# Projections of a gated mLSTM and convolution layer: pairs of tiles by seven block products, all ahead of the mLSTM

## The chip, the cores and the metric

The kernel runs on one core of one Trainium2 chip. The metric is the device time of one execution in microseconds (us); lower is better. Engines: PE (TensorE, matmuls), DVE (VectorE), ACT (ScalarE), POOL (GpSimd), SP (SyncE, issues most DMAs). All data is float32.

## The reference

One layer on 1024 tokens x 1024 channels. A normalised input is projected once by `w_in` (11 blocks), feeds two mixers, and these are merged:

```
h = rmsnorm(x);  p = h @ w_in
q, k, v, o, i, f, z_a, glu(2), z_b, ga, gb = split(p)
q, k = silu(conv4([q, k]));   hm = mlstm(q, k, v, i, f)       # 4 heads of 256
out_a = sigmoid(o) * headnorm(hm) * silu(z_a);   y_a = out_a @ w_pa
u = conv31(glu_a * sigmoid(glu_b));  u = silu(layernorm(u)) * silu(z_b);  y_b = u @ w_pb
merged = sigmoid(ga) * y_a + sigmoid(gb) * y_b
out = rmsnorm(x + merged @ w_out)
```

Both convolutions are causal and depthwise; layernorm takes its mean and variance over the 1024 channels.

## The kernel before

**Products.** Every float32 operand of a large product is split in two: a high half `hi`, cast by ACT (`split`, L138), and a low half `lo = raw - hi`, subtracted by DVE (L139). `mm3` (L152) makes each product of three passes, hi hi, hi lo and lo hi, added in PSUM (L158). `proj` (L229) makes one tile, 128 output channels x 1024 tokens: 8 blocks of 128 input channels x 3 passes x 2 halves of 512 tokens, so 48 matmuls of 512 columns. The input h lies in SBUF, transposed and split (`hth`, `htl`).

**Order.** For each of four heads: v (`v_item`), two tiles each of q and k (with four conv taps on DVE, then silu), of o and za, and two pairs of GLU tiles gb, ga. A GLU tile starts the long convolution of its channels (`glu_a_item`): 31 instructions on DVE (L341, L344) at a priority 1200 lower, so that the scheduler puts them in wherever DVE has nothing else; its result `acc` goes to `c_dram`, and POOL adds it to a sum `s1`. The mLSTM of a head, in four chunks of 256 tokens, is cut in stages (`mlstm`: scores, keys, values, update, finish), which `mlstm_events` (L543) places between the matmuls of the head's last eight tiles. Its results go to `oa_dram`.

After the heads come the merge gates (`sig_item`, 16 tiles sg), and beside them the layer norm: `token_stat` (L654) sums `s1` over channels by small matmuls with ones, `to_row` (L658) sends the mean to DRAM and back as a row for all partitions, `ln_var` (L677) loads each of 8 channel tiles (`ct`, three buffers), subtracts the mean (L674), squares, and POOL adds (L682); a second statistic gives the deviation. Then zb (8 tiles) with the normalised tiles, y_b and y_a (8 tiles each), and the output projection with the final norm.

Weights are loaded by SP two slots ahead and split one slot ahead. Within an engine, instructions run in the order that the scheduler wrote; `tile` pools make an instruction wait until its buffer's last readers are done.

Of the kernel before, what the change touches and what calls it, by code (L numbers as in the profile page):

```python
# [2 lines left out]

# [6 lines left out]
F32 = mybir.dt.float32  # L10
# [6 lines left out]
P = 128  # L17
# [14 lines left out]
TMP = 2  # L32
VW = DH + 2
SLOT = 4 * (DH + 2 * H)

Q0, K0, V0, O0, IF0, ZA0, GA0_, GB0_, ZB0, MA0, MB0 = (
    0, 1024, 2048, 3072, 4096, 4104, 5128, 6152, 7176, 8200, 9224)


@with_exitstack  # L40
def kernel(ctx: ExitStack, tc: tile.TileContext, x, norm_g, w_in, b_if, conv_qk_w, conv_qk_b,
# [25 lines left out]
    c_dram = dpool.tile([KT, P, S], F32, name="c_dram")  # L67
    oa_dram = dpool.tile([KT, P, S], F32, name="oa_dram")
    sga_dram = dpool.tile([KT, P, S], F32, name="sga_dram")
    sgb_dram = dpool.tile([KT, P, S], F32, name="sgb_dram")  # L70
    r_dram = dpool.tile([H, S], F32, name="r_dram")
    ac_dram = dpool.tile([H, NC], F32, name="ac_dram")
    mu_dram = dpool.tile([2, TT, P], F32, name="mu_dram")

    # constants
# [6 lines left out]
    mask = cpool.tile([P, CS], F32, name="mask")  # L82
    nc.gpsimd.memset(mask, BIG)
    nc.gpsimd.affine_select(mask, mask, pattern=[[1, CS]], compare_op=ALU.is_ge, fill=-BIG, base=0,
                            channel_multiplier=-1)
# [14 lines left out]
    # ---------------------------------------------------------------- weights  # L100
    def w_cm(w, c0):
        def load(raw):
            nc.sync.dma_start(raw[:, 0:KT * P].rearrange("p (k c) -> p k c", k=KT),
                              w[:, c0:c0 + P].rearrange("(k p) c -> p k c", p=P))
        return load, KT * P

    def w_v(h, j):
        n = DH + 2 * H if h == 0 else DH
        rows = slice(j * 4 * P, (j + 1) * 4 * P)

        def load(raw):
            r = raw[:, 0:4 * n].rearrange("p (k c) -> p k c", k=4)
            nc.sync.dma_start(r[:, :, 0:DH], w_in[rows, V0 + h * DH:V0 + (h + 1) * DH].rearrange(
                "(k p) c -> p k c", p=P))
            if h == 0:
                nc.sync.dma_start(r[:, :, DH:n], w_in[rows, IF0:IF0 + 2 * H].rearrange("(k p) c -> p k c", p=P))
        return load, 4 * n

    def w_half(w, c0, j):
        def load(raw):  # L120
            nc.sync.dma_start(raw[:, 0:4 * DH].rearrange("p (k c) -> p k c", k=4),
                              w[j * 4 * P:(j + 1) * 4 * P, c0:c0 + DH].rearrange("(k p) c -> p k c", p=P))
        return load, 4 * DH

    slots = []
    raws = {}
    splits = {}
    done = set()

    def do_load(i):  # L130
        if i < len(slots) and i not in raws:
            load, n = slots[i]
            raw = wpool.tile([P, SLOT], F32, tag="wraw", name=f"wraw{i}", bufs=2)
            load(raw)
            raws[i] = (raw, n)
# [6 lines left out]
    def do_split(i):  # L142
        if i < len(slots) and i not in done:
            done.add(i)
            do_load(i)
            raw, n = raws[i]
            hi = wpool.tile([P, SLOT], F32R, tag="whi", name=f"whi{i}")
            lo = wpool.tile([P, SLOT], F32R, tag="wlo", name=f"wlo{i}")
            split(hi[:, 0:n], lo[:, 0:n], raw[:, 0:n])
            splits[i] = (hi[:, 0:n], lo[:, 0:n])  # L150
# [10 lines left out]
    ht_cm, ht_pool = pool("ht_pool", side="right", reuse_waits="tile")  # L161
    hth = ht_pool.tile([P, KT, S], F32R, name="hth")
    htl = ht_pool.tile([P, KT, S], F32R, name="htl")

    def startup(st_pool):
# [19 lines left out]
        for t in range(TT):  # L185
# [42 lines left out]
    # ---------------------------------------------------------------- projection pieces  # L228
    def proj(i, name, rhs=None):  # L229
        """out^T tile [128 channels, 1024 tokens] of one weight slot; yields between quarters of a half."""  # L230
        do_split(i)
        hi, lo = splits.pop(i)
        wv = [v.rearrange("p (k c) -> p k c", k=KT) for v in (hi, lo)]
        ps = pj(name)
        for hf in range(2):
            sl = slice(hf * 512, (hf + 1) * 512)
            pairs = [((wv[0][:, k, :], wv[1][:, k, :]),
                      (hth[:, k, sl], htl[:, k, sl]) if rhs is None else rhs(k, sl)) for k in range(KT)]
            for k in range(0, KT, 2):
                mm3(ps[:, sl], pairs[k:k + 2], first=k == 0, last=k == KT - 2)  # L240
                yield
        return ps

    state = {}

    # ---------------------------------------------------------------- phase 1 pools
    cv_cm, cv = pool("cv", side="right", reuse_waits="tile")
    s1 = cv.tile([P, S], F32, name="s1")
    h1_cm, h1 = pool("h1", reuse_waits="tile")

    def if_tile():
        return h1.tile([P, TT, 2 * H], F32, name="ift")

    ift = if_tile()

    def v_item(i, h):
        if h == 0:
            state["start"](0)
        else:
            do_split(i)  # L260
            do_split(i + 1)
        n = DH + 2 * H if h == 0 else DH
        vh = h1.tile([P, TT, VW], F32R, tag="vh", name=f"vh{h}")
        vl = h1.tile([P, TT, VW], F32R, tag="vl", name=f"vl{h}")
        nc.gpsimd.memset(vh[:, :, DH:DH + 1].bitcast(F32), 1.0)
        nc.gpsimd.memset(vh[:, :, DH + 1:VW].bitcast(F32), 0.0)
        nc.gpsimd.memset(vl[:, :, DH:VW].bitcast(F32), 0.0)
        state["v"] = (vh, vl)
        if h == 0:
            state["start"](1)  # L270
        w2 = []
        for j in range(2):
            hi, lo = splits.pop(i + j)
            w2.append([a.rearrange("p (k c) -> p k c", k=4) for a in (hi, lo)])
        wpair = lambda k: (w2[k // 4][0][:, k % 4, :], w2[k // 4][1][:, k % 4, :])
        if h == 0:
            for t in range(TT):
                if t:
                    state["start"](t + 1)
                ps = ms(f"v0_{t}")  # L280
                sl = slice(t * P, (t + 1) * P)
                mm3(ps[:, 0:n], [((hth[:, k, sl], htl[:, k, sl]), wpair(k)) for k in range(KT)], lo_last=t < 2)
                split(vh[:, t, 0:DH], vl[:, t, 0:DH], ps[:, 0:DH])
                nc.vector.tensor_copy(ift[:, t, :], ps[:, DH:n])
                yield
            return
        for g in range(2):
            ps = pj(f"v{h}_{g}")
            psv = ps.rearrange("p (t c) -> p t c", t=4)
            for j in range(4):  # L290
                t = g * 4 + j
                sl = slice(t * P, (t + 1) * P)
                mm3(psv[:, j, :], [((hth[:, k, sl], htl[:, k, sl]), wpair(k)) for k in range(KT)])
                yield
            split(vh[:, g * 4:g * 4 + 4, 0:DH], vl[:, g * 4:g * 4 + 4, 0:DH], psv)

    def qk_item(i, h, which, j):
        """which 0: q, 1: k; channel tile j of the head; causal conv of 4 taps and silu."""
        key = ("q", "k")[which]
        if j == 0:  # L300
            state[key] = h1.tile([P, 2, S], F32, tag=key + "raw", name=f"{key}raw{h}")
# [542 lines left out]
```

## Time and profile before

| | |
|---|---|
| median of 3 runs (lowest, highest) | 1290.22 us (1289.82, 1290.43) |
| span of the profiled execution | 1287.4 us |
| PE busy | 1275.8 us, 99% |
| DVE busy | 816.8 us, 63% |
| ACT busy | 456.6 us, 35% |
| POOL busy | 82.0 us, 6% |

The time is the device's for a whole execution; the span is what the hardware profiler recorded of one, from its first to its last instruction. A busy share is a mean over stages that differ, so it says little about a single stage. PE's "busy" counts matmuls in flight, which overlap.

### The profile page before, as it was taken

The page shows a single profiled execution, that of the slowest core. Times are in us where ns is not written, and L with a number is a line of the kernel's source. Part 1 is how long each engine was busy: PE and PEld are TensorE (multiplying, and loading weights), DVE is VectorE, ACT ScalarE, POOL GpSimd, SP SyncE. Part 2 cuts the span into 40 slices and gives each one's busy share as a digit, 9 for nine tenths or more (in the row PEclk, how much of TensorE's full clock was granted, in tenths as well). Part 3 has the DMA queues.
Part 4 walks back from the last instruction along what each step waited for, and adds up shares of the span by engine and source line. Part 5 has one row for each costly group of instructions (what it writes and reads, how often), then busy time and mean ns, then how long its engine had stood idle before and what let it go on. Part 6 is the DMA issues. An engine that isn't in the chain of part 4 may idle for free.

```text
span 1287.4 us, 16051 instructions
## 1 busy us (share of the span) xinstructions
PE 1275.8 (99%) x6636; PEld 1079.1 (84%) x6636; DVE 816.8 (63%) x1008; ACT 456.6 (35%) x626; POOL 82.0 (6%) x122
## 2 busy tenths in 40 slices
PE   8999999999999999999999999999999999999997
PEld 7888889888889888898888888888888888888997
DVE  6783479995499984799964899262155333344433
ACT  5565441345431444423454211141333211212224
POOL 1000000001000100001010001050000000000002
PEclk9999999999999999999999999999999999999999
DMA  7112121211111221212121123464332344333403
GB/s 219 45 48 53 46 58 42 82 50 58 54 54 50 66 70 37 66 41 66 49 74 50 42 90 115 133 227 127 102 98 82 115 144 137 96 99 98 180 18 132
DMA packets 121495, 109.82 MB, mean 85 GB/s; under 512 B 4945, under 2 KB 109769, under 8 KB 121422
## 3 DMA queue, kind: packets, MB, share of 16 engines
q1 hardware_dynamic: 121422, 108.80, 27.7%
q8 instruction: 52, 0.85, 0.3%
q14 instruction: 21, 0.17, 0.0%
HBM read 87.79 MB, written 21.00 MB: 84 GB/s over the span
## 4 chain that ended last, share of the span: by engine, by line
PE 96%; ACT 1%; DVE 1%; POOL 1%; DMA 0%; issue 0%; SPq 0%; POOLq 0%; ACTq 0%
PE sg L158 14%; PE o L158 7%; PE zb L158 7%; PE k L158 7%; PE ya L158 7%; PE q L158 7%; PE ga L158 7%; PE za L158 7%; PE gb L158 7%; PE yb L158 7%; PE v L158 6%; PE out L158 6%; PE sc L158 2%; PE ip L158 1%; PE up L158 1%; PE np L158 1%
## 5 line engine op out<-in xcount | busy, mean ns | idle before, releaser
L344 DVE SCALAR_TENSOR_TENSOR acc<-u,dww,acc 128x1024 f32<-128x1024 f32 x240 | 307.5, 1307 | 2.9
L138 ACT CAST whi<-wraw 128x1024 fp32r<-128x1024 f32 (+1 forms) x104 | 109.1, 1049 | 372.6 <-PE sg L158 110.6
L139 DVE TENSOR_TENSOR wlo<-wraw,whi 128x1024 fp32r<-128x1024 f32 (+1 forms) x104 | 130.8, 1257 | 78.8 <-ACT whi L138 78.4
L158 PE MATMUL sg<-hth,whi 128*128 128x512 f32 x256 | 101.5, 396 | 0.0
L158 PE MATMUL sg<-hth,wlo 128*128 128x512 f32 x256 | 101.5, 396 | 0.0
L158 PE MATMUL sg<-htl,whi 128*128 128x512 f32 x256 | 100.7, 393 | 0.0
L158 PE MATMUL out<-whi,mrg 128*128 128x256 f32 x512 | 90.8, 280 | 0.0
L158 PE MATMUL ya<-oa,whi 128*128 128x512 f32 x256 | 80.4, 395 | 0.0
L158 PE MATMUL yb<-u,whi 128*128 128x512 f32 x256 | 80.0, 394 | 0.0
L158 PEld LDWEIGHTS out<-whi,mrg 128*128 128x128 f32 x512 | 78.6, 189 | 0.0
L158 PE MATMUL v<-whi,hth 128*128 128x256 f32 (+1 forms) x256 | 71.7, 289 | 2.0 <-ACT hth L138 2.0
L158 PE MATMUL out<-wlo,mrg 128*128 128x256 f32 x256 | 72.0, 281 | 0.0
L158 PE MATMUL v<-whi,htl 128*128 128x256 f32 (+1 forms) x256 | 70.0, 282 | 0.4 <-DVE htl L139 0.4
L158 PE MATMUL v<-wlo,hth 128*128 128x256 f32 (+1 forms) x256 | 69.9, 281 | 0.0
L158 PEld LDWEIGHTS sg<-hth,wlo 128*128 128x128 f32 x256 | 48.3, 189 | 11.9
L158 PEld LDWEIGHTS yb<-u,whi 128*128 128x128 f32 x256 | 48.4, 189 | 11.6 <-DVE u L139 0.3
L158 PEld LDWEIGHTS sg<-htl,whi 128*128 128x128 f32 x256 | 48.0, 187 | 11.7
L158 PEld LDWEIGHTS ya<-oa,whi 128*128 128x128 f32 x256 | 48.0, 188 | 11.4
L158 PEld LDWEIGHTS sg<-hth,whi 128*128 128x128 f32 x256 | 48.1, 188 | 11.0
L158 PE MATMUL ga<-hth,whi 128*128 128x512 f32 x128 | 51.3, 401 | 0.0
L158 PE MATMUL za<-hth,whi 128*128 128x512 f32 x128 | 51.2, 400 | 0.0
L158 PE MATMUL gb<-hth,whi 128*128 128x512 f32 x128 | 50.9, 397 | 0.0
(234 smaller groups left out, 2984.7 us busy)
## 6 DMA issues: line engine op xcount, KB each, us to landing
wraw<-in_w_in_dram SPq DMA_DIRECT2D x80, 512.0 KB, 4.1
ct<-c_dram SPq DMA_DIRECT2D x16, 512.0 KB, 4.6
xt<-in_x_dram SPq DMA_DIRECT2D x8, 512.0 KB, 4.2
oa_dram<-ot SPq DMA_DIRECT2D x16, 256.0 KB, 2.1
c_dram<-acc SPq DMA_DIRECT2D x8, 512.0 KB
sgb_dram<-sg_s SPq DMA_DIRECT2D x8, 512.0 KB, 2.6
sga_dram<-sg_s SPq DMA_DIRECT2D x8, 512.0 KB, 3.0
wraw<-in_w_pb_dram SPq DMA_DIRECT2D x8, 512.0 KB, 4.5
```

Source lines behind the costliest of these rows:

```text
L138: ins = nc.scalar.copy(hi, src)
L139: nc.vector.tensor_tensor(lo, src, hi.bitcast(F32), op=ALU.subtract)
L158: nc.tensor.matmul(ps, a, b, start=(first and j == 0), stop=(last and j == len(todo) - 1))
L344: nc.vector.scalar_tensor_tensor(acc, u[:, k:k + S], dw(k, c), acc, op0=ALU.mult, op1=ALU.add)
```

## The change

**Block products.** Two tiles of 128 channels (`jobs`, 36 pairs) are made at once. Weights and h are each cut in 2 x 2 blocks (512 input channels x 128 output channels; 512 x 512 tokens), and `quad` (L401) makes the pair from seven products of 12 matmuls (`product`) in place of eight, after Strassen and Winograd, with sums of blocks as operands, and additions on the way out of PSUM by ACT and DVE. Sums of h (`sums`) are made once, during v of heads 2 and 3. Sums of weights are made for each job (`prep`), a job ahead, on DVE.

**Low halves.** Of summed weights, DVE does not subtract: ACT writes hi and then -hi into `lo`, and a DMA of POOL's queue adds the sum to it.

**Order.** All projections come first: v, then four groups of eight jobs (gb, ga, and six of q, k, o, za, mb, ma), then four of zb. q, k, v, gates and the normalised u go to DRAM. The sum over tiles of the long convolution is added up in DRAM by DMAs, the squares of the layer norm in SBUF by DMAs, with two `ct` buffers. The layer norm stands in the last two jobs before zb. Then come the 16 chunks, heads alternating in pairs, with quarters of y_b between the stages, then y_a and the output as before.

```diff
+            if dma:
+                nc.scalar.copy(hi, src)
+                nc.scalar.activation(lo, hi.bitcast(F32), AF.Copy, scale=-1.0)
+                nc.gpsimd.dma_start(lo, src, accum_op=ALU.add)
+            else:
+                split(hi, lo, src)
...
+        a11, a12 = pair("a", raw[:, 1:3])
+        sm = [wq.tile([P, 2, 512], F32, tag="sum", name=f"sum{n}_{i}", bufs=2) for i in range(2)]
+        nc.vector.tensor_tensor(sm[0][:, 0], raw[:, 0], raw[:, 3], op=ALU.add)
+        nc.vector.tensor_tensor(sm[0][:, 1], sm[0][:, 0], raw[:, 1], op=ALU.add)
+        yield
+        s1, s2 = pair("t", sm[0], DMA_LOW)
+        nc.vector.tensor_tensor(sm[1][:, 0], raw[:, 0], raw[:, 1], op=ALU.add)
+        nc.vector.tensor_tensor(sm[1][:, 1], sm[0][:, 1], raw[:, 2], op=ALU.add)
+        yield
+        s3, s4 = pair("s", sm[1], DMA_LOW)
+        yield
+        (a22,) = pair("b", raw[:, 3:4])
...
+    def product(ps, a, b, first, last):
+        for k in range(4):
+            for p, q in PASSES:
+                nc.tensor.matmul(ps, a[p][:, k, :], b[:, q, k, :], start=(first and k == 0 and p == 0 and q == 0),
+                                 stop=(k == 3 and p == 1), skip_group_check=True)
...
+        X, Z = bank("x"), bank("z")
+        product(X, a11, b11, True, False)
+        yield
+        nc.scalar.copy(dst(0, 0), X)
+        product(Z, s1, t1, True, False)
+        yield
+        nc.scalar.copy(dst(1, 1), Z)
+        product(X, s2, t2, False, False)
+        yield
+        nc.scalar.copy(dst(0, 1), X)
+        W = bank("w")
+        product(W, a12, b21, True, True)
+        yield
+        nc.vector.tensor_tensor(dst(0, 0), W, dst(0, 0), op=ALU.add)
+        emit(0, 0, dst(0, 0), False)
+        product(X, s3, t3, False, False)
+        yield
+        nc.vector.scalar_tensor_tensor(dst(1, 1), X, -1.0, dst(1, 1), op0=ALU.mult, op1=ALU.subtract)
+        emit(1, 1, dst(1, 1), False)
+        product(Z, s4, b22, False, True)
+        yield
+        nc.vector.tensor_tensor(dst(0, 1), Z, dst(0, 1), op=ALU.add)
+        emit(0, 1, dst(0, 1), False)
+        product(X, a22, t4, False, True)
+        yield
+        emit(1, 0, X, True)
...
+                    nc.gpsimd.dma_start(s1_dram, acc, accum_op=ALU.add)
...
+                nc.scalar.activation(ct, ct, AF.Square)
+                nc.gpsimd.dma_start(sv, ct, accum_op=ALU.add)
...
+    for n in range(4, first_zb - 2):
+        run_job(n)
+    close(cv_cm)
+    ln_cm, state["lnp"] = pool("lnp", reuse_waits="tile")
+    ln = layer_norm()
+    for n in range(first_zb - 2, first_zb):
+        run_job(n, ln)
...
+    chunks = [mlstm(h, c) for g in (0, 2) for c in range(NC) for h in (g, g + 1)]
...
+            for f in (at(i - 1, "v"), at(i - 1, "u"), at(i + 2, "l"), at(i, "s"), None, at(i, "k"), at(i + 1, "p"), None,
+                      at(i - 2, "f"), None, at(i, "i")):
+                yield f
```

On DVE, in the first head before, the taps of the long convolution (`acc`) run between splits of weights (`wlo`) and of the mLSTM's operands (`kl`, `ql`, `pl`) and its decay matrix (`dm`):

```order
L139 TENSOR_TENSOR kl_0_3800<-kraw_3644,kh_0_3799 128x512
L344 SCALAR_TENSOR_TENSOR acc_3264<-u_3261,dww,acc_3264 128x1024
L139 TENSOR_TENSOR wlo_3954<-wraw_3787,whi_3953 128x1024
L344 SCALAR_TENSOR_TENSOR acc_3264<-u_3261,dww,acc_3264 128x1024 x5
L450 TENSOR_TENSOR dm_0_3805<-sc_0_3889,dm_0_3805 128x384
```

On DVE in a job of the first group now (`f` the pair's results, `w`, `x`, `z` its PSUM banks, `sum` the sums of weights, `raw` the loaded weights):

```order
L103 TENSOR_TENSOR lo11a<-raw_2234,hi11a 128x1024
L422 TENSOR_TENSOR f_0_2239<-w_2282,f_0_2239 128x512
L498 TENSOR_SCALAR acc_1662<-u_1505,dww,par 128x1024
L500 SCALAR_TENSOR_TENSOR acc_1662<-u_1505,dww,acc_1662 128x1024
L426 SCALAR_TENSOR_TENSOR f_1_2240<-x_2241,f_1_2240 128x512
L500 SCALAR_TENSOR_TENSOR acc_1662<-u_1505,dww,acc_1662 128x1024 x2
L430 TENSOR_TENSOR f_0_2239<-z_2242,f_0_2239 128x512
L500 SCALAR_TENSOR_TENSOR acc_1662<-u_1505,dww,acc_1662 128x1024
L198 TENSOR_TENSOR sum_0_2429<-raw_2364 128x512
L500 SCALAR_TENSOR_TENSOR acc_1662<-u_1505,dww,acc_1662 128x1024
L103 TENSOR_TENSOR lo11b<-raw_2234,hi11b 128x512
L199 TENSOR_TENSOR sum_0_2429<-sum_0_2429,raw_2364 128x512
```

The additions out of PSUM (L422, L426, L430) stand among the taps, and the sums for the next job (L198, L199) in the same queue behind them.

On PE around the second layer norm statistic (`tstat`) before, with `sg` the merge gates:

```order
L158 MATMUL sg_6977<-htl,whi_6926 128x512
L158 MATMUL sg_6977<-hth,wlo_6927 128x512
L654 MATMUL tstat_7035<-ones,sv 128x2 x8
L158 MATMUL sg_7047<-hth,whi_6984 128x512
L158 MATMUL sg_7047<-htl,whi_6984 128x512
```

The same place on PE now (`hi38s` and the like are weights of jobs 38 and 39, the last two of zb, `x` and `z` their banks):

```order
L398 MATMUL z_6387<-hb,lo39t 128x512
L398 MATMUL z_6387<-hb,hi39t 128x512 x2
L398 MATMUL z_6387<-hb,lo39t 128x512
L549 MATMUL tstat_5930<-ones,sv 128x2 x8
L555 MATMUL trow_5942<-ident,tst_5939 8x128
L398 MATMUL z_6250<-hb,hi38s 128x512 x2
L398 MATMUL z_6250<-hb,lo38s 128x512
L398 MATMUL z_6250<-hb,hi38s 128x512 x2
```

The statistic has moved from the middle of the merge gates to the last two jobs; products 1 and 2 of job 39 stand ahead of it, products 6 and 7 of job 38 behind it.

## Rows read from the trace of the kernel before

**Rows 1.** The page: span, busy by engine, DVE by slices, chain by engine
```profile
span 1287.4 us, 16051 instructions
PE 1275.8 (99%) x6636; PEld 1079.1 (84%) x6636; DVE 816.8 (63%) x1008; ACT 456.6 (35%) x626; POOL 82.0 (6%) x122
...
DVE  6783479995499984799964899262155333344433
...
PE 96%; ACT 1%; DVE 1%; POOL 1%; DMA 0%; issue 0%; SPq 0%; POOLq 0%; ACTq 0%
```

**Rows 2.** Windows: length, busy of PE, PEld, DVE, ACT, POOL, clock, DMA, GB/s
```profile
250.00:300.00 50.00, 50.00 (x224) 40.59 (x223) 47.96 (x53) 22.73 (x26) 2.48 (x2) 1.00 0.21 57
1275.00:1280.00 5.00, 5.00 (x45) 5.00 (x44) 1.70 (x4) 2.68 (x6) 1.91 (x4) 1.00 0.40 161
1285.00:1287.00 2.00, 0.00 (x0) 0.00 (x0) 0.00 (x0) 0.00 (x0) 0.00 (x0) 0.50 0.37 152
```

**Rows 3.** The chain that ended last: start, length, what
```profile
47.84 22.13 PE q L158 x95
...
125.48 1.45 PE up L158 x12
...
204.17 22.65 PE v L158 x192
...
828.55 1.68 PE tstat L654 x16
...
897.60 1.68 PE tstat L654 x16
...
921.87 89.53 PE zb L158 x384
1011.40 89.17 PE yb L158 x384
1100.57 89.52 PE ya L158 x384
1190.09 70.84 PE out L158 x600
```

**Rows 4.** DVE by line and tile; the tap row has min/median/max ns
```profile
L139 DVE TENSOR_TENSOR wlo<-wraw,whi 128x1024 fp32r<-128x1024 f32 x102 | 128.3, 1257 | 78.8 <-ACT whi L138 78.4
L754 DVE TENSOR_TENSOR sga<-sga,m 128x512 f32<-128x512 f32 x16 | 10.3, 682 | 0.0
L344 DVE SCALAR_TENSOR_TENSOR acc<-u,dww,acc x240: 1269/1278/3318, 180.2 to 805.2; 128x1024 f32<-128x1024 f32 x120
L341 DVE TENSOR_SCALAR acc<-u,dww,par 128x1024 f32<-128x1024 f32 x8 | 6.5, 807 | 0.0
L139 DVE TENSOR_TENSOR pl<-dm,ph 128x384 fp32r<-128x384 f32 x16 | 8.8, 551 | 0.0
L475 DVE SCALAR_TENSOR_TENSOR kwl<-kt,cols,kwh 128x256 fp32r<-128x256 f32 x24 | 10.5, 478 | 17.7 <-ACT kwh L474 17.7
```

**Rows 5.** ACT by line and shape: count | busy us, mean ns | idle before
```profile
L138 ACT CAST whi<-wraw 128x1024 fp32r<-128x1024 f32 x102 | 107.0, 1049 | 371.3 <-PE sg L158 110.6 <-PE ya L158 65.1 <-PE yb L158 40.5
L442 ACT ACT_TABLE_LOAD x16 | 20.5, 1283 | 20.9 <-DVE dm L441 20.7
L714 ACT ACTIVATE ct<-ct,par 128x1024 f32<-128x1024 f32 x8 | 9.8, 1241 | 30.4 <-DVE ct L713 30.4
```

**Rows 6.** DMA issues: what, queue, count, size, median us to landing
```profile
ct<-c_dram SPq DMA_DIRECT2D x16, 512.0 KB, 4.6
...
sgb_dram<-sg_s SPq DMA_DIRECT2D x8, 512.0 KB, 2.6
```

**Rows 7.** Timeline of DVE: start, length, what, idle before it
```profile
830.27 0.17 DVE L668 TENSOR_SCALAR tst<-tstat 128x8 f32<-128x8 f32 x1 [10.78 <-PE tstat L654]
...
839.46 2.36 DVE L674 TENSOR_TENSOR ct<-ct,mu 128x1024 f32<-128x1024 f32 x2 [7.09 <-DMA mu<-mu_dram]
```

**Rows 8.** Timeline of POOL at the second statistic
```profile
899.56 2.57 POOL L687 TENSOR_TENSOR tst<-tst,half 128x8 f32<-128x8 f32 x1 [30.41 <-DVE tst L686]
```

More of the change, by code (lines that the diff above doesn't have):

```diff
@@ L1 @@
[L1 removed]
 from contextlib import ExitStack, nullcontext
+from itertools import chain, islice
 import concourse.bass as bass
@@ L98 @@
     dw = lambda k, t: dww[:, k * KT + t:k * KT + t + 1]
[L101 to L135, printed above, removed]
     def split(hi, lo, src):
@@ L226, in load_params, with v_job, wpair @@
         nc.vector.tensor_copy(dww, ps[:, 112:360])
[L229 to L275, printed above, removed]
+    ift_cm, ift_pool = pool("ift_pool", reuse_waits="tile")
+    ift = ift_pool.tile([P, TT, 2 * H], F32, name="ift")
+    vt_cm, vt_pool = pool("vt_pool", reuse_waits="tile")
+    def v_job(n, h):
+        j = jobs[n]
+        nv = DH if h else VN
+        v_rows = v_dram[h].rearrange("(g t p) c -> g p t c", g=2, p=P)
+        def wpair(k):
+            hi, lo = j[k // 4]
+            return hi[:, k % 4, :], lo[:, k % 4, :]
         if h == 0:
@@ new lines, in zb_job, with run_job @@
+    def zb_job(n, i):
+        cts = []
+        for j in range(2):
+            ct = centred(2 * i + j, 1)
+            nc.vector.tensor_tensor(ct, ct, state["rstd"], op=ALU.mult)
+            nc.scalar.activation(ct, ct, AF.Silu, bias=lb(2 * i + j), scale=lg(2 * i + j))
+            cts.append(ct)
+        return act_job(n, AF.Silu, store=lambda j: u_dram[2 * i + j], by=lambda j: cts[j])
+    def run_job(n, *others):
+        load(n + 1)
+        side = [prep(n + 1) if n + 1 < len(jobs) else iter(()), *others]
+        for step, _ in enumerate(jobs[n]["fn"](n)):
+            if step > 1:
+                for g in side:
+                    next(g, None)
+        for _ in side[0]:
+            pass
@@ new lines, with start @@
+    st_cm, st_pool = pool("st_pool", reuse_waits="tile")
+    warm = ms("warm")
+    for _ in range(11):
+        nc.tensor.transpose(warm[:, 0:P], ident, ident)
+    state["st"] = st_pool
+    gen = startup(st_pool)
+    def start(t):
+        next(gen, None)
+        if t == 4:
+            load_params(st_pool)
+    state["start"] = start
+    start(0)
+    start(1)
+    run_job(0)
+    close(st_cm)
+    gate_steps = gates()
+    next(gate_steps)
+    run_job(1)
+    next(gate_steps, None)
+    close(vt_cm)
@@ new lines @@
+    cv_cm, state["cv"] = pool("cv", reuse_waits="tile")
+    for n in range(4, first_zb - 2):
[5 more added lines that the diff above has]
+        run_job(n, ln)
+    for _ in ln:
+        pass
+    for n in range(first_zb, len(jobs)):
+        run_job(n)
+    close(ln_cm)
+    close(tmp_cm)
+    close(ext_cm)
+    close(qb_cm)
+    close(wq_cm)
+    close(hb_cm)
+    pj_cm, state["pj"] = pool("pj2_pool", bufs=2, space=PSUM)
@@ new lines, in do_split, with ahead, proj @@
+    def do_split(i):
+        if i < len(slots) and i not in done:
+            do_load(i)
+            done.add(i)
+            hi, lo = [wpool.tile([P, KT * P], F32R, tag=x, name=f"{x}{i}", bufs=3) for x in ("whi", "wlo")]
+            split(hi, lo, raws.pop(i))
+            splits[i] = (hi, lo)
+    def ahead(i, n):
+        for j in range(i, i + n + 1):
+            do_split(j)
+        do_load(i + n + 1)
+    def proj(i, name, rhs):
+        do_split(i)
+        wv = [v.rearrange("p (k c) -> p k c", k=KT) for v in splits.pop(i)]
+        ps = pj(name)
+        for hf in range(2):
+            sl = slice(hf * 512, (hf + 1) * 512)
+            pairs = [((wv[0][:, k, :], wv[1][:, k, :]), rhs(k, sl)) for k in range(KT)]
+            for k in range(0, KT, 2):
+                mm3(ps[:, sl], pairs[k:k + 2], first=k == 0, last=k == KT - 2)
+                yield
+        return ps
@@ new lines @@
+    chunks[0]["l"]()
+    chunks[1]["l"]()
+    do_load(0)
+    chunks[0]["p"]()
+    yb = y_b()
+    ny = 0
+    last = False
+    for i, f in enumerate(stages()):
+        if f is not None:
+            f()
+        elif i > 22:
+            for _ in range(1 if ny % 8 else 1):
+                next(yb, None)
+                if ny % 8 == 0:
+                    ahead(ny // 8, 1)
+                ny += 1
+        if 2 <= i < 2 + KT:
+            u2_tile(i - 2)
+        if i == 12:
+            do_split(0)
```

679 lines of the change are left out of this document (381 added, 298 removed).

## The prediction, written before the changed kernel ran

> **What bounds the kernel now.** I read four views. The page first: PE is busy in 1275.8 of 1287.4 us and holds 96% of the chain that ended last [rows 1]. DVE's mean of 63% hides two regimes; its slices stand at 8 and 9 in the first half, at 2 to 6 later, and in one stretch of 50 us it was busy in 47.96 while PE lost nothing [rows 1, 2]. So DVE was nearly full early on and off the path. Then the chain: it is matmuls from 47.84 us to the end [rows 3]. The zb block gives PE's rate: 384 matmuls of 512 columns in 89.53 us, 0.2332 us each, 11.19 a tile of 48. Third, the groups by line for DVE and ACT, since the change hands them work [rows 4, 5]; last, the DMA list and the timeline around the first statistic [rows 6, 7].
>
> PE's time divides so: 47.84 until q starts; 72 tiles of w_in, 72 x 11.19 = 805.7; three v heads at 22.65, 67.9; yb and ya, 178.7; from 1190.09 to the end 97.3 [rows 3]. 1287.4 less these leaves 90.0: two statistics at 1.68 and 86.6 of chunk matmuls, 5.4 for each of 16 chunks. In the chain a chunk's products (up, 1.45 at 125.48) stand between projection matmuls: these cover the chunks' long hand-overs.
>
> **Part 1: seven products for eight.** 72 tiles of 48 matmuls become 36 jobs of 84: 432 fewer, 432 x 0.2332 = 100.7 us off PE. A job is 19.58 us, a product 2.80. No other PE work goes.
>
> **Part 2: can DVE and ACT feed jobs of 19.58 us?** Per job DVE does one subtraction 1024 wide (1.26), four sums, one subtraction and three PSUM additions 512 wide (0.68 each, the row at that width): 6.7 us. A group of eight jobs has 53.8 of that, 12 conv taps for q and k (15.3), 2 za products (2.5), 2 x 1.4 of GLU products and 62 taps of the long convolution (60 x 1.28 + 2 x 0.81 = 78.4): 152.8 us against PE's 156.6, 97.6% [rows 4]. The slack is 0.48 us a job. Before, DVE in such a state cost nothing [rows 2]; now PE waits for it inside every job: X is added and its bank's next product is two products away, 2.80 us for PE's end, DVE's queue and 0.68, with a tap of 1.28 in front at worst. The first order rows show where DVE itself stops: L198 writes a sum tile that the accumulating DMA of the pair before still reads, and the taps behind it wait too. That DMA starts after product 4, one hi cast and one negation on ACT (2.1 us, 3.4 with a table load [rows 5]) and takes D.
>
> D is not in the trace. Bounds: a plain store of the same 512 KB takes 2.6, and load and store one after the other 4.6 + 2.6 = 7.2 [rows 6]; I take 5, next to the load, since it reads both sides. On the Trainium skill, page DMA: Bandwidth & Descriptors, section Anatomy of one DMA — SWDGE (gpsimd) path: its fit for a descriptor-generated transfer would make 3.2 us of 512 KB, an estimate by that page for a plain copy. No run here shows one that adds; by it this part's loss would be 5 in place of 22, and the total some 22 us lower.
>
> With D = 5 the sum tile is free 7.5 to 9 us after product 4, and DVE is there 6.4 to 7.7 after it: 1.1 us of wait a job, 0.65 over the slack. Over the 33 jobs with taps: **+22 us**. With D = 2.6 it is about 5 (table loads alone), with 7.2 some 60.
>
> **Part 3: layer norm.** Before it ran beside 16 sg tiles: statistics at 828.55 and 897.60, 69 us apart, with no gap on PE [rows 3]. Now the glu jobs come every eighth, the last taps end with job 35, and the statistics fall in the last three jobs; the second order rows show PE meeting the second statistic with products of jobs 38 and 39 behind it. The chain, from the first statistic's end T0: mean, row to DRAM and back, 9.2 (830.27 to 839.46 [rows 7]). Then eight steps on two tiles in place of three, each load 4.6, subtract 1.2, square 1.05 (as a cast of that width), accumulating DMA 5, and some 0.08 a hand-over; a tile returns after 12.1, two of them make 6.05 a step. The first load lies beside the row, so 7.5 steps: the sums are complete at T0 + 54.6. Second statistic 1.7, square root 2.57 on POOL [rows 8], row 9: T0 + 68. Normalise (1.26), Silu (1.28 of table and 1.24), one product (1.26) and one store of 2.6, with their hand-overs, free the f tile that job 38's product 6 needs, at T0 + 77. Then 7 products at 2.80: zb ends at T0 + 96.4. PE's own work in that time is 47.3 (8.1 of job 37 and two jobs), so it stands 49; with 2.8 at the first statistic, less 1.7 for the second that the old time also had, **+50 us**. With D = 2.6 a step is 4.85, some 10 us less; with 7.2 it is 7.15, 9 more. The transfers of weights beside it are cover that PE doesn't use.
>
> **Part 4: chunks without projections.** All 16 chunks now run after zb, with q, k, v and the gate loaded again, 64 quarters of y_b (11.19 / 8 = 1.40 each) three to a slot as the only filler, from slot 2. PE's work is 86.6 + 89.5 = 176. DVE's instructions of a slot by width (512: 0.68, 384: 0.55, 256: 0.48 and below [rows 4]) come to about 9.2, and to 9.5 to 14.1 in the first six, which also split u2 (1.26 each): 154.5 over the 15 intervals from the first scores to the last. PE has about 9.8 in a slot with three quarters, 5.6 without. The longer of the two, slot by slot, sums to 164; a tenth more for the hand-overs PE, DVE, ACT, PE inside one chunk (v needs the split of the scores, up that of the keys, 0.5 to 1 us each): 180. Before it 4.5 for loads and splits after zb; behind it 25 quarters and the last chunk, 39, and 9 until the last outputs are stored, reloaded (4.6) and split (1.05 + 1.26). 232 against 176: **+56 us**. From below: at 8% over PE's own work as the filler covers nearly all, +24; from above, twice the hand-over share and a slot of 13: +80.
>
> **Other edits, at nothing.** Token sums lie beside v heads 2 and 3 (DVE there has no taps yet). The y_a and out blocks are the old ones, with m1 loaded from DRAM in 4.6 us two tiles ahead; if that cover goes it is under 5 in all. Stores of q, k, v, gates on SP: 512 KB each at 2.6, well below a job.
>
> **The sum.** The profiled execution: 1287.4 - 100.7 + 22 + 50 + 56 = 1314.7. The median of the runs shown, 1290.22, lies 2.8 above that span; so **1317 us**.
>
> **Rivals.** A, faster: the hand-overs cost what the queues' sums say and no more. Phase A 5, layer norm 47, chunks +32 (176 to 208, the 164 in place of 180 and half of the reload): 1287.4 - 100.7 + 84 + 2.8 = 1273.5. For it: DVE at 48 of 50 us ran without holding anyone [rows 2], and slots have three chunks in flight. Against: in that stretch nobody waited for DVE. It decides as soon as parts 2 and 4 together stay under 50. The order rows of L198 are what speaks against its first term.
> B, much slower: an accumulating DMA of 9 us, past the sum of load and store, since it must read, add and write per packet. Part 2: the wait for the sum tile grows by up to 4 a job; PE, held too, moves product 4 back by about half, so (5.1 - 0.48) / 2 = 2.3 x 33 = 76; the seven serial steps of layer norm add about 25: 1287.4 - 100.7 + 76 + 75 + 56 + 2.8 = 1396. With the other parts as forecast, the change loses from D of about 2.6 on (1317 - 17 - 10 = 1290).
> C, the clock: in the last stretch, with PE stopped, the granted clock read 0.50, and 1.00 ten us earlier with PE full [rows 2]; the slots of part 4 leave PE a quarter idle, and layer norm leaves it still for tens of us. If half of part 4's work ran at 1.2 GHz, 88 us of it would double, some 33 of that inside waits: +55, 1372. The Trainium skill, page TensorE: Matmul & The Clock Gate, section Part 1: The HAM clock gate, says that the clock falls when PE idles and comes back with sustained work; the row of 0.50 agrees, but no row here shows a partly busy PE at the low level.
> That fewer products are issued is not open: the order has 3024 matmuls at L398 where there were 3456.
>
> **How the numbers follow.** Forecast 0.53, own range 1294 to 1350 (parts 2, 3, 4 from 10, 42, 40 to 40, 58, 68, not all at one end). A 0.28, from 1255 to 1294. B 0.10, C 0.09. A measurement of this kernel tells 0.2%, 2.6 us, from no change. Faster by more: nearly all of A, 0.25; within, 0.03, where A and the forecast meet; slower 0.72. The range for 8 in 10 takes in A's upper two thirds and C's edge: 1263 to 1376.
>
> **What would show it.** Right: L398's matmuls at 0.233 us in 84s and jobs of 20.0 to 20.5 in phase A with PE's gaps released by DVE at L422 or L426, and DVE's by a POOL DMA at L198; PE idle about 28 us before the second statistic and 18 before job 38's product 6; slots of 10 to 12 us with DVE the releaser. Wrong: jobs of 19.6 (A), accumulating DMAs far from 5 us, a clock at 0.50 between 750 and 1150, or gaps of PE at steps that I cost at nothing.

## The result: 4.1% slower, and the profile after

The changed kernel takes 1343.11 us (median of 4 runs, 1340.09 to 1343.83) against 1290.33 us before it on the same chip: ratio 1.0406, 95% interval 1.0391 to 1.0420. The forecast was 1317 us, slower; the time lies 26 us above that, inside its range of 1294 to 1350.

The page of the changed kernel's profile: span, busy time by engine, three of its slices.

```profile
span 1341.1 us, 16597 instructions
PE 1219.2 (91%) x6204; PEld 1025.1 (76%) x6204; DVE 947.3 (71%) x1250; ACT 624.4 (47%) x916; POOL 121.7 (9%) x229
...
PE   8999999999999999989999998255898999899997
...
DVE  6882499798998979989798983247886763344433
...
PEclk9999999999999999999999898666899999899999
```

Against [rows 1], PE is busy 57 us less, but no longer from end to end: its slices fall to 2 and 5 two thirds of the way, and there the granted clock falls too, which before happened only after PE's last work [rows 2]. DVE's slices now stand at 7 to 9 through nearly the whole projection phase. In units of time, by stage on PE (the stages cut at starts of PE's instructions, PE's work at full speed as the forecast reckoned it, 19.58 us a job):

| stage | PE's work at full speed | forecast loss | measured | loss |
|---|---|---|---|---|
| start to the first pair job | 115.8 | 0 | 124.3 | 8.5 |
| 33 jobs to the fourth from the end | 646.1 | 22 | 669.1 | 23.0 |
| last three jobs, statistics included (3.4) | 62.1 | 50 | 119.4 | 57.3 |
| mLSTM, y_b and y_a | 265.5 | 56 | 328.1 | 62.6 |
| output and tail | 97.3 | 0 | 100.2 | 2.9 |

The losses sum to 154.3; less the 100.7 of fewer matmuls that is 53.6, and 1287.4 + 53.6 = 1341.0, the span. The three large losses of the forecast are all there; the surplus is 8.5 at the start, 7 each in the layer norm and the mLSTM, 1 in the projection phase, and 2.9 at the end.

Windows of the changed kernel, columns as in [rows 2]: the steady projection phase, a single wait of PE in it, the layer norm, the first part of the mLSTM.

```profile
124.30:793.40 669.10, 650.27 (x2772) 524.82 (x2773) 575.78 (x613) 355.29 (x437) 62.93 (x78) 0.99 0.61 147
...
420.00:424.00 4.00, 1.08 (x5) 0.56 (x3) 4.00 (x5) 0.63 (x1) 0.00 (x0) 0.99 0.45 84
424.00:428.00 4.00, 3.79 (x10) 3.05 (x11) 3.96 (x6) 3.25 (x4) 0.87 (x1) 0.59 0.01 4
...
873.00:880.00 7.00, 3.94 (x17) 3.57 (x17) 1.07 (x3) 0.00 (x0) 1.67 (x1) 0.50 0.23 75
880.00:891.00 11.00, 0.00 (x0) 0.00 (x0) 5.23 (x5) 2.54 (x3) 0.00 (x0) 0.50 0.33 124
...
920.00:926.00 6.00, 3.73 (x16) 3.23 (x16) 3.27 (x4) 1.82 (x4) 0.00 (x0) 0.50 0.89 279
```

The second and third of these show the price of a short wait: PE stood for 3.1 us, and in the next 4 us the clock was 0.59 with PE busy in 3.79 of them. Adding up PE's busy time x (1 - granted clock) over windows of 1 us gives the time that the low clock added to PE's work, 34 us in the whole run: 8 in the projection phase, 10 in the last three jobs, 16.5 in the mLSTM and the beginning of y_a.

What PE waited for, all told (engine, operand, releaser: us in total, times, longest):

```profile
PE tstat L549 <- DMA sv<-ct: 18.8, 1, 18.8
PE x L398 <- DVE f L426: 15.2, 8, 3.5
PE z L398 <- ACT f L415: 12.4, 1, 12.4
PE z L398 <- DMA lo39t<-sum: 7.2, 1, 7.2
PE sc L112 <- ACT kh L102: 7.2, 1, 7.2
PE tstat L549 <- DMA s<-s_dram: 6.5, 1, 6.5
...
PE gT L363 <- ACT gst L355: 2.2, 1, 2.2
PE x L398 <- ACT vt L312: 2.2, 1, 2.2
...
PE ifT L329 <- DVE ift L298: 1.2, 1, 1.2
```

The first, third, fourth and sixth lines are the layer norm, the second is the subtraction from X in the jobs, the fifth the start of the mLSTM, and the last three lie ahead of the first pair job. The DMAs of the layer norm, and one of the 72 that add the sums of weights, in the columns of [rows 6]:

```profile
ct<-c_dram SPq DMA_DIRECT2D x16, 512.0 KB, 5.1
...
s_dram<-acc POOLq DMA_DIRECT2D x7, 512.0 KB, 8.6
sv<-ct POOLq DMA_DIRECT2D x7, 512.0 KB, 5.5
...
lo10t<-sum POOLq DMA_DIRECT2D x1, 512.0 KB, 4.5
```

Of the 72 for weights 63 land after 4.5 to 5.3 us, the others after up to 8.7; the layer norm's have a median of 5.5. The forecast took 5 for both. Into DRAM it is 8.6 (5.6 to 8.8).

DVE before one of PE's waits in the projection phase (timeline: start, length, what, wait before it):

```profile
409.72 0.68 DVE L203 TENSOR_TENSOR sum<-sum,raw 128x512 f32<-128x512 f32 x1
414.65 0.81 DVE L498 TENSOR_SCALAR acc<-u,dww,par 128x1024 f32<-128x1024 f32 x1 [4.25 <-DMA s_dram<-acc]
415.50 3.93 DVE L500 SCALAR_TENSOR_TENSOR acc<-u,dww,acc 128x1024 f32<-128x1024 f32 x3
419.34 1.22 DVE L103 TENSOR_TENSOR lo19a<-raw,hi19a 128x1024 fp32r<-128x1024 f32 x1
420.48 1.28 DVE L500 SCALAR_TENSOR_TENSOR acc<-u,dww,acc 128x1024 f32<-128x1024 f32 x1
421.67 0.68 DVE L422 TENSOR_TENSOR f<-w,f 128x512 f32<-128x512 f32 x1
422.27 1.28 DVE L500 SCALAR_TENSOR_TENSOR acc<-u,dww,acc 128x1024 f32<-128x1024 f32 x1
423.46 0.68 DVE L426 SCALAR_TENSOR_TENSOR f<-x,f 128x512 f32<-128x512 f32 x1
```

A wait of 4.25 us for the convolution's only tile, then no gap at all up to L426, for which PE stood from 421.1 to 424.2. Waits of 3.6 to 4.7 us with taps close behind come four times, in jobs 14 (for a sum tile), 18, 26 and 34 (for the convolution's tile), and each such job takes 23.5 to 25.2 us. Jobs 11, 12, 20 and 28 take 20.7 to 21.1, most others 19.4. DVE's waits for the convolution's tile, and the groups of the sums in the columns of [rows 4], with 58 us of waits in 36 jobs:

```profile
DVE acc L498 <- DMA s_dram<-acc: 14.8, 4, 4.7
...
L202 DVE TENSOR_TENSOR sum<-raw 128x512 f32<-128x512 f32 x36 | 24.8, 689 | 33.2 <-DMA lo4s<-sum 4.3 <-DMA lo5s<-sum 3.8 <-DMA lo37s<-sum 3.1
L198 DVE TENSOR_TENSOR sum<-raw 128x512 f32<-128x512 f32 x36 | 24.7, 686 | 25.0 <-DMA lo14t<-sum 4.6 <-DMA lo4t<-sum 4.2 <-DMA lo22t<-sum 2.9
```

### The profile page after: what moved, and what is told of

The parts are those of the page before. It is cut to its first block, busy times and chain, and to the rows that moved or that the text cites. A ratio compares the mean times of both kernels' runs of the same rounds, so it can differ in the third digit from the quotient of the medians.

```text
span 1341.1 us, 16597 instructions
## 1 busy us (share of the span) xinstructions
PE 1219.2 (91%) x6204; PEld 1025.1 (76%) x6204; DVE 947.3 (71%) x1250; ACT 624.4 (47%) x916; POOL 121.7 (9%) x229
## 5 line engine op out<-in xcount | busy, mean ns | idle before, releaser
L112 PE MATMUL v<-hi,hb 128*128 128x256 f32 (+1 forms) x512 | 95.2, 289 | 2.5 <-ACT hb L102 2.0
L112 PEld LDWEIGHTS v<-hi,hb 128*128 128x128 f32 x512 | 80.0, 192 | 3.6 <-ACT hb L102 2.6
L448 ACT ACTIVATE f<-f 128x512 f32<-128x512 f32 x72 | 45.4, 630 | 67.4 <-DVE f L426 39.8
L112 PE MATMUL v<-lo,hb 128*128 128x256 f32 (+1 forms) x256 | 71.7, 289 | 0.0
L102 ACT CAST whi<-wr 128x1024 fp32r<-128x1024 f32 x24 | 25.2, 1049 | 76.9 <-PE ya L112 57.4
L470 DVE SCALAR_TENSOR_TENSOR qa<-qr,par,qa 128x1023 f32<-128x1023 f32 (+2 forms) x48 | 59.3, 1277 | 0.0
L112 PE MATMUL ya<-oa,wlo 128*128 128x512 f32 x128 | 52.2, 408 | 0.0
L112 PE MATMUL yb<-u,wlo 128*128 128x512 f32 x128 | 50.8, 397 | 0.0
L112 PEld LDWEIGHTS out<-wlo,mrg 128*128 128x128 f32 x256 | 49.1, 192 | 0.0
L112 PEld LDWEIGHTS v<-lo,hb 128*128 128x128 f32 x256 | 48.4, 193 | 0.0
L202 DVE TENSOR_TENSOR sum<-raw 128x512 f32<-128x512 f32 x36 | 24.8, 689 | 33.2 <-DMA lo4s<-sum 4.3
L198 DVE TENSOR_TENSOR sum<-raw 128x512 f32<-128x512 f32 x36 | 24.7, 686 | 25.0 <-DMA lo14t<-sum 4.6
```

What stands on the lines that cost most here:

```text
L198: nc.vector.tensor_tensor(sm[0][:, 0], raw[:, 0], raw[:, 3], op=ALU.add)
L202: nc.vector.tensor_tensor(sm[1][:, 0], raw[:, 0], raw[:, 1], op=ALU.add)
L448: nc.scalar.activation(t[j][:, HF[hf]], src, func, scale=sgn(neg))
L470: nc.vector.scalar_tensor_tensor(acc[j][:, s:], raw[j][:, 0:S - s], cw(KQ - 1 - s, t), acc[j][:, s:], op0=ALU.mult, op1=ALU.add)
```

## The experiments

All times are medians with the kernel before at 1289.9 to 1290.3 us beside them; ratios are to it, with 95% intervals. "Projection phase" ("phase A" in the expectations) is the stretch of 669.1 us above. In the code `...` marks lines left out.

**Early release of the convolution's tile.**

```diff
...
-                    nc.gpsimd.dma_start(s1_dram, acc, accum_op=ALU.add)
+                    nc.gpsimd.dma_start(s1_dram, c_dram[c], accum_op=ALU.add, max_dma_last_dim=S)
```

> The tile that a long convolution adds up in has one buffer, and its next first tap waits until the accumulating DMA into the sum in DRAM (8.6 us to landing) has read it. Here that DMA reads the stored copy in DRAM, so the tile is free after its plain store. Theory (the buffer sets the four stalls): DVE's waits of 4.2 to 4.7 us at the first taps of the odd channels go, PE's four stalls of 3.1 to 3.5 us at the subtraction from X go, and with them the stretches at half clock behind them (1.6 to 3.0 us each). 4 x (3.3 + 2) = 21 us less; the last sum is complete some 3 us later, so 16 to 20 us less in all: 1323 to 1327 us, jobs at 19.4 to 19.9 us throughout. Rival (DVE is simply full, as the forecast had it): the time saved is lost again at the next additions, no more than 5 us less: 1338 to 1343 us.

Measured 1340.87 us, ratio 1.0392 (1.0361 to 1.0423): no difference from the changed kernel. The wait at L498 is gone and the projection phase takes 669.1 us as before: other waits of DVE stand in its place, the longest for the sum tiles (in the changed kernel 2.9, 2.7 and 4.6),

```profile
DVE sum L198 <- DMA lo22t<-sum: 7.0, 1, 7.0
DVE sum L198 <- DMA lo30t<-sum: 5.4, 1, 5.4
DVE sum L198 <- DMA lo14t<-sum: 4.8, 1, 4.8
```

and the long jobs are 14, 22 and 30 (23.6 to 25.6 us) in place of 14, 18, 26 and 34. The theory of the one tile falls; the rival's number holds.

**Low halves of the sums by DVE** (`DMA_LOW = False`).

> The low halves of the summed weights by one subtraction on DVE, as for the other weights, in place of negation and accumulating DMA. DVE gets 2 x 1.14 us a job at its real pace and loses its waits for the sum tiles (58 us over 36 jobs, 1.6 a job). Theory (DVE has slack once the overlap of its instructions is counted): 0.7 us a job more against some 0.2 of slack left, 33 x 0.5 = 16: 1348 to 1363 us. Rival of the forecast (DVE 97.6% full): 2.5 - 0.48 a job, +66, 1400 us or more. Second rival (the accumulating DMAs were the trouble): faster than 1335 us.

Measured 1387.93 us, 1.0762 (1.0745 to 1.0778): 45 us slower than the change, between the two first expectations. The projection phase grows by only 12.8 us, but the last tap of the long convolution starts at 855.2 us, 59 later than in the changed kernel:

```profile
L500 DVE SCALAR_TENSOR_TENSOR acc<-u,dww,acc x240: 1272/1282/1289, 166.4 to 855.2; 128x1024 f32<-128x1024 f32 x120
```

From the first pair job to the last tap DVE is busy 666.9 us in place of 578.3, 88.6 more, and stands 29.5 less, since its waits at the sum tiles are gone and others grew: 59 together. Nothing of the added work went into slack; only the waits that it replaced made room for it. So DVE is full, its waits counted in.

**Extra matmuls at two waits**, behind the row of the second statistic and ahead of the first scores; nothing reads their results.

```diff
+            idle_fill("b", 26, dww, tr)
...
+    idle_fill("c", 16, dww, state["mm"])
```

> Extra matmuls whose result nothing reads stand in PE's order at two waits: 26 behind the second layer norm row, ahead of the last two products of the job before last, and 16 ahead of the first scores of the mLSTM (each some 0.42 us at full clock; the waits there were 12.4 and 7.2 us). Theory (PE's idling lowers the granted clock, and that stretches the work behind it): the clock stands at 1.00 behind both, 1.7 us less in the last zb products and 4 to 8 us less in the first 45 us of the mLSTM: 1331 to 1338 us. Rival (the clock is low there because DVE and ACT starve PE slot by slot, and PE's pace is not what sets the slots): within 2 us of 1343, or slower by what the extra matmuls overrun.

Measured 1341.92 us, 1.0401 (1.0383 to 1.0418): no difference. The clock stood at 1.00 behind the first of them, and at 0.98 to 1.00 for 10 us behind the second, but then fell as before:

```profile
891.00:915.00 24.00, 24.00 (x107) 19.91 (x106) 14.87 (x16) 12.14 (x17) 2.84 (x9) 1.00 0.64 203
...
920.00:930.00 10.00, 6.14 (x46) 5.45 (x46) 8.70 (x16) 7.82 (x14) 0.17 (x3) 0.98 1.05 332
930.00:940.00 10.00, 4.30 (x18) 3.85 (x19) 9.23 (x17) 9.20 (x18) 1.10 (x3) 0.50 0.81 275
```

The last zb products took 1.5 us less (19.8 for 21.3), as the theory has it, and 4 to 8 us in the first slots did not come: from the first scores to the output the stretch is 321 us in both kernels. In the mLSTM the low clock still added 14.3 us where it had added 16.5, so the run tests the clock over the first slots alone. There what it stretched lay inside what the waits allow.

**Squares summed early.** In the long convolution's end, and the pass over eight tiles taken out:

```diff
...
+                sq = cv.tile([P, S], F32, tag="sq", name=f"sq{c}", bufs=1)
+                nc.scalar.activation(sq, acc, AF.Square)
...
+                    nc.gpsimd.dma_start(s2_dram, sq, accum_op=ALU.add)
...
+        m2 = lnp.tile([P, TT], F32, name="m2")
+        nc.vector.tensor_tensor(m2, st, st, op=ALU.mult)
...
+        ps, st = token_stat(s2, 1)
         nc.vector.tensor_scalar(st, ps, 1.0 / D, EPS, op0=ALU.mult, op1=ALU.add)
+        nc.vector.tensor_tensor(st, st, m2, op=ALU.subtract)
```

> The sum of squares of the layer norm is added up during the convolutions, as the sum is (a square on ACT and an accumulating DMA into DRAM for each tile), and the variance is the mean square less the squared mean; the pass of eight tiles between the two statistics is gone. Theory (that serial pass is what PE waited for): PE's waits of 18.8, 12.4 and 7.2 us go, with the half clock around them; the deviation's row is there some 18 us after the first statistic in place of 76. 45 to 55 us less: 1288 to 1298 us. Rival (the wait moves to the next link, the row through DRAM and the last tiles' normalisation): about 20 us less, 1323 us.

Measured 1303.66 us, 1.0101 (1.0084 to 1.0118): 39 us less, where 45 to 55 were expected. Of PE's waits at the layer norm one is left,

```profile
PE tstat L556 <- DMA s<-s_dram: 9.4, 1, 9.4
```

so the serial pass was the cause of the others. That one grew by 2.9 us, and the projection phase takes 3.6 us longer.

**A third sum tile, and the early release.**

```diff
-        sm = [wq.tile([P, 2, 512], F32, tag="sum", name=f"sum{n}_{i}", bufs=2) for i in range(2)]
+        sm = [wq.tile([P, 2, 512], F32, tag="sum", name=f"sum{n}_{i}", bufs=3) for i in range(2)]
...
-        ct = state["lnp"].tile([P, S], F32, tag="ct", name=f"ct{n}_{c}", bufs=2)
+        ct = state["lnp"].tile([P, S], F32, tag="ct", name=f"ct{n}_{c}", bufs=1)
...
```

> Phase A alone is asked about (start of the first pair job to start of the fourth from the end, 669.1 us in the changed kernel and 669.1 with the early release of the convolution's tile alone). Both things that DVE waits for there are relaxed: the convolution's tile is free after its plain store, and the sums of weights get a third buffer; to pay for it the layer norm's tile loses its second, which makes the layer norm longer by 25 to 40 us. Theory (DVE's waits of 4 to 5 us for a DMA, at one tile or the other, are what makes it late at X): the waits at the sum tiles go too, phase A falls to 645 to 652 us. Rival (the order is simply too dense while taps last, waits or not): 660 us or more.

One run, 1399.39 us, the layer norm's single tile included; the projection phase takes 681.3 us, not 645 to 652. DVE now meets the first sum of a job before its weights have landed:

```profile
DVE sum L198 <- DMA raw<-in_w_in_dram: 60.3, 24, 9.2
```

Its waits at L202 stay too, 31.6 us in the phase where they were 27.6. So this did not test what it was to test: the waits were moved to the loaded weights, which have two buffers, not removed. The rival's number is met without its reason being shown.

**Half the taps.** (`range(1, KD)` becomes `range(1, 16)`.)

> The long convolution runs 16 of its 31 taps; the other 15 are left out. Phase A again. DVE's work in a group of eight jobs falls by 2 x 15 x 1.19 = 36 us, while the accumulating DMAs and the single buffer stay. Theory (waits hurt only because taps stand close behind them): stalls at X go, phase A 640 to 648 us. Rival (the waits hurt by themselves): 660 us or more, with DVE idle far over 12%.

One run, 1299.53 us. The layer norm starts in job 34 here and lies in the projection phase as it was cut (672.6 us), so the numbers of the expectation don't apply as they stand, and the 30 jobs up to there are compared: 589.9 us in place of 604.8, at 19.4 a job 582. Two thirds of the loss is gone, as the theory has it, with every accumulating DMA and the single tile still in place. Windows of this kernel over the stretch in which the changed kernel's DVE was busy in 230.6 of 260 us:

```profile
202.00:462.00 260.00, 258.21 (x1116) 208.92 (x1116) 171.73 (x196) 144.19 (x182) 26.66 (x34) 1.00 0.66 160
```

At 66% DVE's waits cost PE next to nothing, at 89% they do.

**No filler between the stages** (`elif i > 22` never true).

> No quarter of y_b stands between the stages of the mLSTM; all 64 follow the last chunk. The changed kernel takes 178 us from the first scores to the last, 11.9 a slot, with PE's own work at 5.4 + 4.2 a slot. Theory (DVE's work and the hand-overs set a slot, the filler rides along): 9 to 10 us a slot without filler, 135 to 150 us for the 15, then 89.5 for y_b instead of about 35: 10 to 30 us slower, 1352 to 1372. Rival (PE's work sets the slots): 6 to 7 us a slot, about 100, and a total within 5 us of 1343 or below.

Measured 1362.59 us, 1.0566 (1.0548 to 1.0584): 19 us slower than the change. The mask of the scores, once a chunk, in this kernel and then in the changed one:

```profile
L764 DVE TENSOR_TENSOR dm<-sc,dm x16: 534/550/553, 923.8 to 1067.9; 128x384 f32<-128x384 f32 x16
```

```profile
L764 DVE TENSOR_TENSOR dm<-sc,dm x16: 536/551/553, 924.5 to 1101.0; 128x384 f32<-128x384 f32 x16
```

144.1 / 15 = 9.6 us a slot without filler, 11.8 with it. Over these slots DVE is busy 8.1 us of the 9.6:

```profile
923.80:1067.90 144.10, 110.29 (x743) 95.70 (x744) 122.16 (x293) 98.25 (x219) 21.57 (x84) 0.94 0.63 200
```

PE's own products, 5.4 us a slot at full pace and 7.4 in flight here, don't set the slot; the theory's number holds. How the 9.6 divides between DVE's work and the hand-overs is not shown, and the filler adds 2.2 to it.

**Four buffers for the loads of the last phases** (tag "st", bufs 2 to 4).

> The tile through which u, the outputs of the mLSTM and the merge gates are loaded from DRAM gets four buffers in place of two. In the changed kernel the last outputs come one by one (load 3.2 to 4.3, cast 1.05, subtraction 1.24) while y_a has begun: 8 us of waits of PE between 1135 and 1162 us and 5 us lost to the clock. Theory (two buffers make that chain serial): those 10 to 13 us go, and the first slots, which load u through the same tile, gain 0 to 4: 1328 to 1334. Rival (the loads wait for the last chunks' own stores): no more than 3 us less.

Measured 1331.41 us, 1.0324 (1.0308 to 1.0339): 12 us less, as the theory has it. The output begins at 1228.2 in place of 1240.9 us.

**Both gains together, with q and k of the fourth head last in their group.**

```diff
...
-        for name, fn, base, h in rest[6 * i:6 * i + 6]:
+        for name, fn, base, h in (rest[6 * i:6 * i + 6] if i < 3 else rest[20:24] + rest[18:20]):
...
```

> Three edits at once: the sum of squares during the convolutions (40 us faster than the changed kernel by itself), four buffers for the loads from DRAM in the last phases (12 us by itself), and in the last group of eight jobs q and k of the fourth head after o, za, mb, ma, so that their 12 conv taps come behind the long convolution's. Theory (the first two are different places on PE, so they add; the third lets the long convolution end up to 15 us earlier, and of the 20 us that PE still loses around the statistics half goes): 1343 - 40 - 12 - 5 to 10: 1281 to 1288 us. Rival (the gains overlap, or q and k late collide with the layer norm on DVE): 1292 us or more.

Measured 1296.30 us, 1.0049 (1.0037 to 1.0061). The expectation is missed by 8 to 15 us: the last tap did not come earlier, but starts at 809.0 us in place of 799.3 with the squares alone (795.9 in the changed kernel), and 39 + 12 became 47. Three edits at once do not say which of them cost the difference.

**The last tile apart.**

```diff
...
+        c7 = lnp.tile([P, S], F32, tag="ct", name="c7", bufs=2)
+        nc.sync.dma_start(c7, c_dram[KT - 1])
+        ps, st = token_stat((s1, c7), 0)
...
```

> As the kernel with three edits, and the last tile of the long convolution is not added up in DRAM: it is loaded after its plain store, and the statistics sum it on PE beside the sum of the other seven. The wait before the first statistic was 9.4 us with accumulating DMA (9.6 with its issue) and reload (5) in a row. Theory (that chain sets the wait): 5 to 7 us less there, 3.4 us more of small matmuls: 2 to 4 us less than the kernel with three edits. Rival (with the earlier end of the convolution the statistic waits for nothing any more): 3 us more than that kernel.

Measured 1291.19 us, 1.0010 (0.9997 to 1.0022): 5 us less than the kernel with three edits, where 2 to 4 were expected; it is the best version, and level with the kernel before. The wait at the first statistic fell from 5.3 to 0.7 us.

**X copied out by ACT**, on the change and on the best version.

```diff
-        nc.vector.scalar_tensor_tensor(dst(1, 1), X, -1.0, dst(1, 1), op0=ALU.mult, op1=ALU.subtract)
+        nc.scalar.copy(dst(1, 0), X)
+        nc.vector.scalar_tensor_tensor(dst(1, 1), dst(1, 0), -1.0, dst(1, 1), op0=ALU.mult, op1=ALU.subtract)
```

> The changed kernel with one edit: after product 5, ACT copies X out of its bank (into the quarter of the result that product 7 will fill), and DVE subtracts from that copy. Product 7 then waits for a copy on ACT and no longer for DVE's place in its queue; DVE's late subtraction may come up to two products later before PE feels it, by way of ACT's queue. Theory (DVE is late by 2 to 5 us now and then, whichever DMA it waited for, and PE's allowance of one product at X turns that into time): the waits at the subtraction (18.5 us in all) and the half clock behind them (8 us in phase A) go, jobs at 19.4 to 19.8; phase A 669 to 645-652 us, 16 to 24 us less in all: 1319 to 1327 us. Rival (DVE is short of time as such): the waits move to the next bank or to the next job's weights, phase A 660 us or more, 1336 to 1343 us.

> The same edit on the kernel with the last tile apart (1291.2 us, four mends), whose phase A still holds 25 us of waits and 7 us lost to the clock. Theory as for the edit alone: 16 to 26 us less, 1265 to 1275 us, 1.2 to 2.0% faster than before the change. Rival (DVE short of time): 1284 to 1291 us.

Measured 1348.46 us, 1.0444 (1.0423 to 1.0466), and 1295.82 us, 1.0061 (1.0037 to 1.0084): each median 5 us above that without it, so both theories fall, and the times lie above the rivals' ranges too. The projection phase takes 668.8 us on the change (in the fastest of its four executions, 1341.66 us, so what the others lost is not in the trace) and 680.7 on the best version, which had 674.1. PE's wait has only changed its name, and ACT, whose next function reads what DVE adds up, hands it on (waits of PE, then of ACT, in the first of the two):

```profile
PE x L398 <- ACT f L426: 20.7, 8, 4.1
...
ACT f L449 <- DVE f L427: 41.6, 23, 4.2
ACT f L449 <- DVE f L422: 40.0, 13, 5.2
```

## Why the prediction was right, point by point

**Fewer matmuls, 100.7 us:** as forecast; a job without waits takes 19.4 us where 19.58 was reckoned.

**Projection phase, +22 forecast, +23.0 measured: the right engine and the right kind of wait, and the size in part by luck.** The step said that DVE is at 97.6% and that its wait at L198 for the accumulating DMA tips it over by 0.65 us in every job. D was sized well (5 against 4.5 to 5.3 for most). But there is no 0.65 in every job: most jobs run at full rate, and eight take 1.3 to 5.8 us more, where DVE has waited and the taps leave it no gap to catch up before X. Against the 19.4 us of a job without waits the loss is 28.9 and not 23.0: 18.5 of PE's waits, 8 of the low clock behind them, which the step did not have, and some 2 besides.

The load was also reckoned too high. Most instructions start before the one ahead has ended (behind a tap of 1.28 us another instruction starts 1.20 after the tap's start; only a tap behind a tap starts later, after 1.32), so DVE is busy in 575.8 of 669.1 us, 86%. Waits fill the rest, 89 us: 43 at the sum tiles for the accumulating DMAs, 1.3 a job where the forecast had 1.1, but 28 of them at L202, which it did not name; 14.8 for the accumulating DMA at the convolution's tile, which it put at nothing and which stands ahead of three of the four long jobs; 17 for ACT. Only 13 us are waits for PE, and these are all the slack that DVE had.

That the stream is full is shown three ways: 88.6 us more of work put the last tap 59 us later, half the taps give two thirds of the loss back, and with one wait removed, or one link of PE's chain to DVE, the phase still takes 669.1 and 668.8 us. Which waits would have to go together to break this is open: third buffers for weights and sums at once were not tried.

The Trainium skill's fit for a transfer by POOL's queue (DMA: Bandwidth & Descriptors, section Anatomy of one DMA — SWDGE (gpsimd) path) gave 3.2 us as an estimate; the traces have 4.5 to 5.3 for most that add into SBUF and a median of 8.6 for those that add into DRAM, so the bound from load and store was the better guide.

**Layer norm, +50 forecast, +57.3 measured: the mechanism right, two terms short.** From the first statistic's end (814.9) to the second's start (873.1) the trace has 58.2, the forecast 54.6; zb ends 97.9 after, forecast 96.4. The 7 are a first wait of 6.5 for 2.8, since the sum's DMA goes to DRAM at 8.6 and not 5; 1.9 at the first statistic, 3.57 for 1.68, at a granted clock of 0.50 behind that wait; and 1.5 in the chain behind it, in which the second statistic took 3.57 too, at 0.50 again:

```profile
811.33 3.57 PE L549 MATMUL tstat<-ones,s 128*128 128x2 f32 x16 [6.53 <-DMA s<-s_dram]
...
873.10 3.57 PE L549 MATMUL tstat<-ones,sv 128*128 128x2 f32 x16 [18.84 <-DMA sv<-ct]
...
891.47 1.22 PE L398 MATMUL z<-hb,hi38s 128*128 128x512 f32 x2 [12.41 <-ACT f L415]
```

The last line answers the forecast that product 6 of job 38 waits for a tile held by the store of u. The wait for `lo39t` (7.2 us, shown above) stands ahead of the second statistic, for which PE then waited 18.8 us more, so it cost nothing of its own. Taking the serial pass out gave 39 us back.

**mLSTM and y_b, +56 forecast, +62.6 measured: right in size, the cause in part argued.** First scores 7.2 us after zb's end (4.5), 178 us from there to the last scores (180), 53.3 behind them (48). The run without filler shows that a slot takes 9.6 us of its 11.8 without any product of y_b, so PE's own work does not set it. How much of this is DVE, hand-overs, the new loads from DRAM (between the first scores and the last, ACT waits 11.6 us for k) or the low clock, no run separates. The 5 behind the last scores are the loads of the outputs two at a time, which the forecast put into 9 us; four buffers gave 12 back, more than the term.

**At nothing:** the start was not. The first pair job begins at 124.3 us: waits of 1.2 and 2.2 for the gates' transposes, and 2.2 until the v tile's banks are free, are 5.6 of the 8.5 us. That no other products stand ahead of them now is the likely reason; no run shows it. The other 2.9, and the 2.9 of the output and tail, were not traced.

**The clock (rival C, 0.09)** is real, and smaller than C had it. The granted clock falls to 0.50 behind the four longest waits of the projection phase, 2.3 to 3.5 us, and behind those of the layer norm; behind the waits of 0.5 to 1.5 us in that phase, and behind one of 2.6 in the mLSTM, it stayed at 1.00. The Trainium skill (TensorE: Matmul & The Clock Gate, section Part 1: The HAM clock gate) has it that idling lowers the clock; the trace agrees. The low clock added 34 us to PE's work, 16.5 of them in the mLSTM and the beginning of y_a, where C reckoned 88. With the clock held up at two places the time was the same; over most of the mLSTM, and in the projection phase, where it rides on DVE's waits, it was not tried alone. Rival A fell with the 23 and 62.6. Rival B's 9 us was near for the DMAs into DRAM, but not for those it spoke of, into SBUF.

## What to carry to other kernels

An engine off the path that is busy 86 to 89% of the time, as DVE here, is no reserve once the path is made to wait for it several times in each job (at 66% it was one): what counts is its stream with its waits, in order, and where a single wait was removed here the next ones filled its place. When work is taken from the busiest engine, price first what that work covered: here projections covered the mLSTM's hand-overs and the layer norm's serial pass, and of 100.7 us won all was given back and 53 more. A serial pass of DMAs can be spread over the phase before it; here that alone was worth 39 us.

## What the runs showed of the hardware

- DVE: behind a tap of 1.28 us (128 x 1024) another instruction starts 1.20 us after the tap's start, but the next tap, which adds to the same tile, 1.32 after it. Most instructions 512 wide last 0.68 us, and the next starts after 0.60.
- After a wait of PE of 3.1 us the granted clock over the next 4 us was 0.59, and 1.00 in the 4 us behind these.
- A DMA that adds 512 KB took 4.5 to 5.3 us into SBUF in 63 of 72 cases for weights (up to 8.7 in the others), and 8.6 (median) from SBUF into DRAM.
